# Head-wise expert routing on one Trainium2 core: three of eight blocks as a block diagonal, and transpositions dealt out between the expert blocks

## The chip, the cores and the metric

The kernel runs on one core of one Trainium2 chip. The metric is the device time of one execution in microseconds; lower is better. All data are fp32.

## What is computed

`x` has 64 x 1024 rows of 1024 numbers, seen as 16 heads of 64. Each row is routed to one head by the largest of 16 logits, and only that head is transformed and kept; all others are zero in the output.

```python
route_logits = x @ route_w                 # [B, S, 16]
best_head = np.argmax(route_logits, axis=-1)
x_heads = x.reshape(B, S, H, Dh)           # H = 16, Dh = 64
for h in range(H):
    mask = (best_head == h)
    out[:, :, h, :] = np.matmul(x_heads[:, :, h, :], experts[h]) * mask[:, :, None]
```

The kernel computes every head's product densely and multiplies by the mask.

## The kernel before

The 65536 rows are cut into 512 tiles of 128 rows (128 x 1024 fp32, 512 KB). SyncE's queue loads each tile into `xin` (20 buffers, line 87) and stores each output tile from `ot` (10 buffers, line 145). A tile's 1024 columns are eight blocks of 128, and each block holds two heads.

`transpose_tile` turns the eight blocks with TensorE (line 96), four into each of two PSUM buffers `ps_t`, and ScalarE copies each four to `xt` in SBUF (line 97). The transposed block is the stationary operand of the next step.

`expert_tile` takes each block `p` as four matmuls in 64x64 sub-arrays of TensorE (line 112): the upper and the lower 64 channels (two heads, `half`) times the first and the last 64 rows (`th`). The moving operand `mv` is 64 x 80: the head's 64x64 expert beside the 16 columns of `route_w` for those channels. Even blocks hold the expert first and then the routing columns, odd ones the other way round, so that the routing columns of a pair fall on the same 16 PSUM columns and add up there. Upper heads go to `ps_a` (two buffers, two banks each), lower heads to `ps_b` (one buffer, two banks). So 32 matmuls per tile.

Then VectorE adds up the partial logits (two reductions, line 120, and an addition, line 127), finds the maximum and its index (129, 131), makes the mask (133), and multiplies the upper heads from PSUM into `ot` (143). ScalarE copies the lower heads to `raw` (124), and GpSimd multiplies those into `ot` (144).

The order on TensorE follows the program: all eight transpositions of tile j, then all matmuls of tile j-1, and so on. The framework puts in the waits between engines from the buffers' use. Each fp32 expert matmul is recorded as two matmul records with a weight load each, a transposition as one.

Of the kernel before, what the change touches and what calls it, by code (L numbers as in the profile page):

```python
# [1 line left out]

# [5 lines left out]

FP32 = mybir.dt.float32
I32 = mybir.dt.int32  # L10
U32 = mybir.dt.uint32
ALU = mybir.AluOpType
AX = mybir.AxisListType

P = 128
XIN_BUFS = 20
OUT_BUFS = 10
XT_BUFS = 3


@with_exitstack
def kernel(
    ctx: ExitStack,
    tc: tile.TileContext,
    x: bass.AP,
    route_w: bass.AP,
    experts: bass.AP,
    out: bass.AP,
):

    nc = tc.nc
    B, S, D = x.shape  # L40
    H = experts.shape[0]
    Dh = D // H
    N = B * S
    NB = D // P
    NT = N // P
    HB = 512
    W = Dh + H
    assert D % P == 0 and N % P == 0 and Dh * H == D and 2 * Dh == P and NB == 8

    xg = x.rearrange("b s d -> (b s) d").rearrange("(g p) d -> g p d", p=P)  # L50
    og = out.rearrange("b s d -> (b s) d").rearrange("(g p) d -> g p d", p=P)

    consts = ctx.enter_context(tc.tile_pool(name="consts", bufs=1))
    small = ctx.enter_context(tc.tile_pool(name="small", bufs=3))
    xin_pool = ctx.enter_context(tc.tile_pool(name="xin", bufs=XIN_BUFS))
    xt_pool = ctx.enter_context(tc.tile_pool(name="xt", bufs=XT_BUFS))
    raw_pool = ctx.enter_context(tc.tile_pool(name="raw", bufs=3))
    out_pool = ctx.enter_context(tc.tile_pool(name="outp", bufs=OUT_BUFS))
    ps_t_pool = ctx.enter_context(tc.tile_pool(name="ps_t", bufs=2, space=bass.MemoryType.PSUM))
    ps_a_pool = ctx.enter_context(tc.tile_pool(name="ps_a", bufs=2, space=bass.MemoryType.PSUM))  # L60
    ps_b_pool = ctx.enter_context(tc.tile_pool(name="ps_b", bufs=1, space=bass.MemoryType.PSUM))

    ident = consts.tile([P, P], FP32, name="ident")
    make_identity(nc, ident)


    mv = consts.tile([P, NB, W], FP32, name="mv")
    ev = experts.rearrange("(q ab two) d e -> two ab d q e", two=2, ab=2)
    rv = route_w.rearrange("(q ab k) h -> ab k q h", k=P, ab=2)
    mvv = mv.rearrange("k (q ab) w -> k ab q w", ab=2)  # L70
    with nc.allow_non_contiguous_dma(reason="constants, once"):
        for ab in range(2):
            e0, r0 = (0, Dh) if ab == 0 else (H, 0)
            for half in range(2):
                nc.scalar.dma_start(
                    out=mvv[half * Dh:(half + 1) * Dh, ab, :, e0:e0 + Dh], in_=ev[half, ab])
            nc.scalar.dma_start(out=mvv[:, ab, :, r0:r0 + H], in_=rv[ab])  # L77


    hid_i = consts.tile([P, H], I32, name="hid_i")  # L80
    nc.gpsimd.iota(hid_i, pattern=[[1, H]], base=0, channel_multiplier=0)  # L81
    hid = consts.tile([P, H], FP32, name="hid")
    nc.vector.tensor_copy(out=hid, in_=hid_i)  # L83

    def load(j):
        xin = xin_pool.tile([P, D], FP32, name="xin", tag="xin")
        nc.sync.dma_start(out=xin, in_=xg[j])
        return xin

    def transpose_tile(xin):  # L90
        xt = xt_pool.tile([P, NB, P], FP32, name="xt", tag="xt")
        for half in range(2):
            ps_t = ps_t_pool.tile([P, NB // 2, P], FP32, name="ps_t", tag="ps_t")
            for q in range(NB // 2):
                p = half * (NB // 2) + q
                nc.tensor.transpose(ps_t[:, q, :], xin[:, p * P:(p + 1) * P], ident)  # L96
            nc.scalar.copy(out=xt[:, half * (NB // 2):(half + 1) * (NB // 2), :], in_=ps_t)  # L97
        return xt

    def windows(ps):  # L100

        return ps[:, :, 0:2 * W].rearrange("k q (ab w) -> k q ab w", ab=2)[:, :, :, 0:Dh]

    def expert_tile(j, xt):
        ps_a = ps_a_pool.tile([P, NB // 2, HB // 2], FP32, name="ps_a", tag="ps_a")
        ps_b = ps_b_pool.tile([P, NB // 2, HB // 2], FP32, name="ps_b", tag="ps_b")
        for p in range(NB):
            q, ab = divmod(p, 2)
            o0 = ab * Dh
            for half, ps in ((0, ps_a), (1, ps_b)):  # L110
                for th in range(2):
                    nc.tensor.matmul(  # L112
                        ps[th * 64:(th + 1) * 64, q, o0:o0 + W],
                        lhsT=xt[half * 64:(half + 1) * 64, p, th * 64:(th + 1) * 64],
                        rhs=mv[half * 64:(half + 1) * 64, p, :],
                        start=(p % 4 == 0), stop=(p % 4 == 3), skip_group_check=True)

        lg2 = small.tile([P, 2, H], FP32, name="lg2", tag="lg2")
        for half, ps in ((0, ps_a), (1, ps_b)):
            nc.vector.tensor_reduce(  # L120
                out=lg2[:, half, :], in_=ps[:, :, Dh:W].rearrange("k q h -> k h q"),
                op=ALU.add, axis=AX.X)
        raw = raw_pool.tile([P, NB // 2, 2, Dh], FP32, name="raw", tag="raw")
        nc.scalar.copy(out=raw, in_=windows(ps_b))  # L124

        lg = small.tile([P, H], FP32, name="lg", tag="lg")
        nc.vector.tensor_add(out=lg, in0=lg2[:, 0, :], in1=lg2[:, 1, :])  # L127
        mx = small.tile([P, 8], FP32, name="mx", tag="mx")
        nc.vector.max(out=mx, in_=lg)  # L129
        ix = small.tile([P, 8], U32, name="ix", tag="ix")  # L130
        nc.vector.max_index(out=ix, in_max=mx, in_values=lg)  # L131
        mask = small.tile([P, H], FP32, name="mask", tag="mask")
        nc.vector.tensor_scalar(  # L133
            out=mask, in0=hid, scalar1=ix[:, 0:1], scalar2=None, op0=ALU.is_equal)

        ot = out_pool.tile([P, D], FP32, name="ot", tag="ot")
        ov = ot.rearrange("k (q ab two e) -> k two q ab e", two=2, ab=2, e=Dh)
        mk = mask.rearrange("k (q ab two) -> k two q ab", two=2, ab=2)

        def bc(half):  # L140
            return mk[:, half].unsqueeze(3).to_broadcast([P, NB // 2, 2, Dh])

        nc.vector.tensor_tensor(out=ov[:, 0], in0=windows(ps_a), in1=bc(0), op=ALU.mult)  # L143
        nc.gpsimd.tensor_tensor(out=ov[:, 1], in0=raw, in1=bc(1), op=ALU.mult)  # L144
        nc.sync.dma_start(out=og[j], in_=ot)

    prev = None
    for j in range(NT + 1):
        xt = transpose_tile(load(j)) if j < NT else None
        if prev is not None:  # L150
            expert_tile(j - 1, prev)
        prev = xt


# [1 line left out]
_INS = ['x', 'route_w', 'experts']  # L156
_OUTS = [((64, 1024, 1024), 'float32')]


# [23 lines left out]
```

## Time and profile before

| what | value |
|---|---|
| median of 14 runs | 1646.59 us (1636.57 to 1663.43) |
| the profiled execution | 1641.88 us, its span 1640.1 us |
| TensorE, VectorE, ScalarE, GpSimd busy | 82%, 59%, 50%, 33% of the span |
| mean granted TensorE clock | 0.949 |
| data DMA (queue 1) | 536.94 MB, 90.8% of 16 engines' span |
| HBM traffic | 268.76 MB read, 268.44 MB written, 328 GB/s |

In the profile's rows PE is a matmul on TensorE and PEld a weight load, which can run beside it. DVE is VectorE, ACT ScalarE, POOL GpSimd, SP SyncE. L96 is line 96 of the kernel. "issue" is time in which an engine waited for nothing that the profile shows. The clock is the share of full TensorE clock that was granted.

### The profile page before, as it was taken

The numbers are of one execution on the slowest core, as the hardware profiler recorded it, in microseconds if no ns is written. First come the engines' busy times: TensorE is split into PE (matmuls) and PEld (weight loads), VectorE is DVE, ScalarE is ACT, GpSimd is POOL, SyncE is SP. The second block draws the span as 40 slices with busy tenths as digits, with TensorE's granted clock in tenths as the row PEclk, the third lists the DMA queues.
The fourth block names the chain that finished last, engine by engine and source line by source line (L and its number), as shares of the span: only waits on it lengthen the run. The fifth ranks groups of instructions, "written<-read, shape, count | busy, mean of one in ns | idle before, by whom it ended". The sixth has DMA issues, their size and how long they took to land.

```text
span 1640.1 us, 85016 instructions
## 1 busy us (share of the span) xinstructions
PE 1341.9 (82%) x36864; PEld 1168.6 (71%) x36864; DVE 965.2 (59%) x4097; ACT 812.5 (50%) x1537; POOL 537.6 (33%) x519
## 2 busy tenths in 40 slices
PE   7778888888888788788888888878878887888888
PEld 6667776767777677677777777767767776777777
DVE  4555555556556566565566565556555655656566
ACT  4444545445445555454455454545444544545555
POOL 2233333333333333333333333323333333333333
PEclk9899999999999999999999999999999999999999
DMA  9999999999999899999999999989999899999975
GB/s 348 352 359 362 328 344 328 320 340 337 317 332 356 314 347 355 335 334 334 338 339 344 337 337 334 337 310 330 324 332 343 322 310 345 356 313 338 340 257 208
DMA packets 149974, 542.70 MB, mean 331 GB/s; under 512 B 18528, under 2 KB 18528, under 8 KB 149600
## 3 DMA queue, kind: packets, MB, share of 16 engines
q1 hardware_dynamic: 147456, 536.94, 90.8%
q8 instruction: 290, 4.75, 1.2%
q14 instruction: 84, 0.69, 0.1%
q10 hardware_dynamic: 2144, 0.33, 0.1%
HBM read 268.76 MB, written 268.44 MB: 328 GB/s over the span
## 4 chain that ended last, share of the span: by engine, by line
PE 81%; issue 17%; ACT 1%; DVE 1%; DMA 0%; POOLq 0%; ACTq 0%; DVEq 0%
PE ps_t L96 34%; PE ps_a L112 27%; PE ps_b L112 20%; DVE lg L120 0%; ACT xt L97 0%; ACT raw L124 0%; DMA mv<-in_experts_dram 0%; ACT L97 0%; POOLq L178 0%; DVE lg L127 0%; DVE ix L131 0%; DVE mask L133 0%; DVE ot L143 0%; DVE mx L129 0%; ACTq L77 0%
## 5 line engine op out<-in xcount | busy, mean ns | idle before, releaser
L144 POOL TENSOR_TENSOR ot<-raw,mask 128x512 f32<-128x512 f32 x512 | 536.8, 1049 | 1098.3 <-ACT xt L97 857.4
L112 PE MATMUL ps_a<-mv,xt 64*64 64x80 f32 x16384 | 762.4, 241 | 119.4 <-issue 115.6
L112 PE MATMUL ps_b<-mv,xt 64*64 64x80 f32 x16384 | 756.8, 241 | 113.9 <-issue 109.4
L112 PEld LDWEIGHTS ps_a<-mv,xt 64*64 64x64 f32 x16384 | 651.1, 139 | 222.6 <-issue 145.9
L112 PEld LDWEIGHTS ps_b<-mv,xt 64*64 64x64 f32 x16384 | 646.3, 139 | 127.8 <-issue 122.9
L124 ACT COPY raw<-ps_b 128x512 f32<-128x512 f32 x512 | 300.2, 586 | 755.1 <-DVE lg L120 749.5
L96 PE MATMUL ps_t<-ident,xin 128*128 128x128 f32 x4096 | 600.0, 292 | 58.7 <-issue 52.3
L97 ACT COPY xt<-ps_t 128x512 f32<-128x512 f32 x1024 | 558.0, 596 | 61.4 <-PE ps_t L96 59.0
L96 PEld LDWEIGHTS ps_t<-ident,xin 128*128 128x128 f32 x4096 | 469.3, 148 | 114.8 <-issue 67.2
L120 DVE TENSOR_REDUCE lg<-ps_a 128x16 f32<-128x64 f32 x512 | 115.0, 225 | 508.9 <-PE ps_b L112 289.0
L143 DVE TENSOR_TENSOR ot<-ps_a,mask 128x512 f32<-128x512 f32 x512 | 354.0, 691 | 19.3 <-DVE mask L133 1.4
L133 DVE TENSOR_SCALAR mask<-hid,ix 128x16 f32<-128x16 f32 x512 | 119.9, 234 | 57.4 <-DVE ix L131 3.7
L120 DVE TENSOR_REDUCE lg<-ps_b 128x16 f32<-128x64 f32 x512 | 110.2, 215 | 31.3 <-PE ps_b L112 31.2
L129 DVE MAX8 mx<-lg 128x8 f32<-128x16 f32 x512 | 91.1, 178 | 17.6
L127 DVE TENSOR_TENSOR lg<-lg 128x16 f32<-128x16 f32 x512 | 89.8, 175 | 17.4
L131 DVE FIND_INDEX8 ix<-mx,lg 128x8 uint32<-128x16 f32 x512 | 86.3, 168 | 0.0
L131 DVE MATCH_VALUE_LOAD ix<-mx,lg 128x8 f32 x512 | 47.2, 92 | 17.7
L97 ACT ACT_TABLE_LOAD x1 | 1.3, 1283 | 5.9 <-DMA mv<-in_experts_dram 5.9
L83 DVE CAST hid<-hid_i 128x16 f32<-128x16 int32 x1 | 0.2, 239 | 1.1 <-POOL hid_i L81 1.1
masks.py:197 POOL MEMSET ident<- 128x128 f32 x1 | 0.2, 205 | 0.3 <-POOLq L167 0.3
masks.py:199 POOL TENSOR_SCALAR_AFFINE_SELECT ident<-ident 128x128 f32<-128x128 f32 x1 | 0.3, 292 | 0.0
L167 POOL MEMSET const-float32-0.0<- 128x1 f32 x1 | 0.1, 99 | 0.2 <-issue 0.2
(4 smaller groups left out, 0.4 us busy)
## 6 DMA issues: line engine op xcount, KB each, us to landing
xin<-in_x_dram SPq DMA_DIRECT2D x512, 512.0 KB, 5.9
out_dram<-ot SPq DMA_DIRECT2D x512, 512.0 KB, 5.7
mv<-in_experts_dram ACTq DMA_DIRECT2D x4, 64.0 KB, 6.4
mv<-in_route_w_dram ACTq DMA_DIRECT2D x2, 32.0 KB, 5.8
```

The costliest lines, as they stand in the source:

```text
L83: nc.vector.tensor_copy(out=hid, in_=hid_i)
L96: nc.tensor.transpose(ps_t[:, q, :], xin[:, p * P:(p + 1) * P], ident)
L97: nc.scalar.copy(out=xt[:, half * (NB // 2):(half + 1) * (NB // 2), :], in_=ps_t)
L112: nc.tensor.matmul(ps[th * 64:(th + 1) * 64, q, o0:o0 + W], lhsT=xt[half * 64:(half + 1) * 64, p, th * 64:(th + 1) * 64], rhs=mv[half * 64 ...
L120: nc.vector.tensor_reduce(out=lg2[:, half, :], in_=ps[:, :, Dh:W].rearrange("k q h -> k h q"), op=ALU.add, axis=AX.X)
L124: nc.scalar.copy(out=raw, in_=windows(ps_b))
L127: nc.vector.tensor_add(out=lg, in0=lg2[:, 0, :], in1=lg2[:, 1, :])
L129: nc.vector.max(out=mx, in_=lg)
L131: nc.vector.max_index(out=ix, in_max=mx, in_values=lg)
L133: nc.vector.tensor_scalar(out=mask, in0=hid, scalar1=ix[:, 0:1], scalar2=None, op0=ALU.is_equal)
L143: nc.vector.tensor_tensor(out=ov[:, 0], in0=windows(ps_a), in1=bc(0), op=ALU.mult)
L144: nc.gpsimd.tensor_tensor(out=ov[:, 1], in0=raw, in1=bc(1), op=ALU.mult)
```

## The change

Blocks 0 to 4 (`NS = 5`) stay as four 64x64 matmuls each. Blocks 5 to 7 (`NF = 3`) become one whole-array matmul each: the stationary operand is the transposed block, 128 x 128, and the moving operand `mf` is 128 x 144, the 16 routing columns beside a block diagonal of the two heads' experts, with zeros elsewhere. A tile's results take three PSUM banks, `ps_e`: upper heads, lower heads, and the three whole blocks; there are two such buffers, and `ps_t` has two banks as before.

The logits are added up by one VectorE reduction over all three banks. ScalarE copies both heads of the five blocks (2 x 352 columns) to `raw`, GpSimd multiplies these by the mask in two operations, and VectorE multiplies the three whole blocks.

The expert matmuls now run two tiles behind the transpositions (`LAG = 2`, four `xt` buffers), and the two are dealt out alternately: one expert block of tile j-2, one transposition of tile j, eight times per step.

```diff
-XT_BUFS = 3
+XT_BUFS = 4
+LAG = 2
...
-    ps_a_pool = ctx.enter_context(tc.tile_pool(name="ps_a", bufs=2, space=bass.MemoryType.PSUM))
-    ps_b_pool = ctx.enter_context(tc.tile_pool(name="ps_b", bufs=1, space=bass.MemoryType.PSUM))
+    ps_e_pool = ctx.enter_context(tc.tile_pool(name="ps_e", bufs=2, space=bass.MemoryType.PSUM))
...
+    mv = consts.tile([P, NS, W], FP32, name="mv")
+    mf = consts.tile([P, NF, STEP], FP32, name="mf")
+    nc.vector.memset(mf, 0.0)
...
+    def transposes(xin, xt):
         for half in range(2):
             ps_t = ps_t_pool.tile([P, NB // 2, P], FP32, name="ps_t", tag="ps_t")
             for q in range(NB // 2):
                 p = half * (NB // 2) + q
                 nc.tensor.transpose(ps_t[:, q, :], xin[:, p * P:(p + 1) * P], ident)
+                if q == NB // 2 - 1:
+                    nc.scalar.copy(out=xt[:, half * (NB // 2):(half + 1) * (NB // 2), :], in_=ps_t)
+                yield
...
+    def experts_pass(ps, xt):
+        for p in range(NS):
+            s, ab = divmod(p, 2)
+            o0 = s * STEP + ab * Dh
+            for half in range(2):
                 for th in range(2):
                     nc.tensor.matmul(
+                        ps[th * 64:(th + 1) * 64, half, o0:o0 + W],
                         lhsT=xt[half * 64:(half + 1) * 64, p, th * 64:(th + 1) * 64],
                         rhs=mv[half * 64:(half + 1) * 64, p, :],
+                        start=(p == 0), stop=(p == NS - 1), skip_group_check=True)
+            yield
+        for f in range(NF):
+            o0 = f * STEP + Dh
+            nc.tensor.matmul(
+                ps[:, 2, o0:o0 + STEP], lhsT=xt[:, NS + f, :], rhs=mf[:, f, :],
+                start=(f == 0), stop=(f == NF - 1), skip_group_check=True)
+            yield
...
+    def finish(j, ps):
+        lg = small.tile([P, H], FP32, name="lg", tag="lg")
+        parts = ps[:, :, 0:SLOTS * STEP].rearrange("k b (s w) -> k b s w", w=STEP)
+        nc.vector.tensor_reduce(
+            out=lg, in_=parts[:, :, :, Dh:W].rearrange("k b s h -> k h b s"),
+            op=ALU.add, axis=AX.XY)
+        RW = (NS // 2) * STEP + Dh
+        raw = raw_pool.tile([P, 2, SLOTS * STEP], FP32, name="raw", tag="raw")
+        nc.scalar.copy(out=raw[:, :, 0:RW], in_=ps[:, 0:2, 0:RW])
...
+        nc.vector.tensor_tensor(
+            out=ov[:, NS:], in1=bc(mk[:, NS:]), op=ALU.mult,
+            in0=ps[:, 2, W:W + NF * STEP].rearrange("k (f w) -> k f w", w=STEP)[:, :, 0:2 * Dh]
+            .rearrange("k f (two e) -> k f two e", two=2))
+        rv4 = raw.rearrange("k two (s w) -> k s two w", w=STEP)
+        for ab in range(2):
+            n = (NS + 1 - ab) // 2
+            o0 = ab * W
+            nc.gpsimd.tensor_tensor(
+                out=ov[:, ab:NS:2], in0=rv4[:, 0:n, :, o0:o0 + Dh], in1=bc(mk[:, ab:NS:2]),
+                op=ALU.mult)
         nc.sync.dma_start(out=og[j], in_=ot)
...
+    for j in range(NT + LAG):
+        tr = mm = iter(())
+        if j < NT:
+            xin = load(j)
+            xts[j] = xt_pool.tile([P, NB, P], FP32, name="xt", tag="xt")
+            tr = transposes(xin, xts[j])
+        if j >= LAG:
+            ps = ps_e_pool.tile([P, SLOTS, HB], FP32, name="ps_e", tag="ps_e")
+            mm = experts_pass(ps, xts.pop(j - LAG))
+        for _ in range(NB):
+            next(mm, None)
+            next(tr, None)
+        if j >= LAG:
+            finish(j - LAG, ps)
```

`W` is 80, `STEP` is 144, `SLOTS` is 3, `HB` is 512 and `NB` is 8.

## The prediction

> **What bounds the kernel now.** I read the page first: engines, chain of waits, groups, queues.
>
> ```profile
> PE 1341.9 (82%) x36864; PEld 1168.6 (71%) x36864; DVE 965.2 (59%) x4097; ACT 812.5 (50%) x1537; POOL 537.6 (33%) x519
> ...
> q8 instruction: 290, 4.75, 1.2%
> ...
> PE 81%; issue 17%; ACT 1%; DVE 1%; DMA 0%; POOLq 0%; ACTq 0%; DVEq 0%
> ...
> L112 PE MATMUL ps_a<-mv,xt 64*64 64x80 f32 x16384 | 762.4, 241 | 119.4 <-issue 115.6
> ...
> L96 PE MATMUL ps_t<-ident,xin 128*128 128x128 f32 x4096 | 600.0, 292 | 58.7 <-issue 52.3
> ```
>
> The chain is TensorE and its own "issue" idle time; every other engine has slack. A transposition is one matmul record (4096 = 512 x 8), an expert matmul two (16384 = 512 x 16 x 2, and as many in ps_b). So a tile has 72 matmul records, and as many weight loads.
>
> Next the timeline, TensorE alone, where the two kinds of work meet. Columns: start, length, instruction, count.
>
> ```profile
> 803.96 0.23 PE L112 MATMUL ps_a<-mv,xt 64*64 64x80 f32 x1
> 803.97 0.24 PE L112 MATMUL ps_b<-mv,xt 64*64 64x80 f32 x2
> 804.14 1.09 PE L96 MATMUL ps_t<-ident,xin 128*128 128x128 f32 x8
> 805.16 0.29 PE L112 MATMUL ps_a<-mv,xt 64*64 64x80 f32 x2
> ```
>
> ```profile
> 808.36 0.29 PE L112 MATMUL ps_a<-mv,xt 64*64 64x80 f32 x2 [0.70 <-DVE mask L133]
> 808.37 0.29 PE L112 MATMUL ps_b<-mv,xt 64*64 64x80 f32 x2
> 808.42 0.29 PE L112 MATMUL ps_a<-mv,xt 64*64 64x80 f32 x2
> 808.49 0.23 PE L112 MATMUL ps_b<-mv,xt 64*64 64x80 f32 x1
> 808.49 0.23 PE L112 MATMUL ps_a<-mv,xt 64*64 64x80 f32 x1
> 808.50 0.23 PE L112 MATMUL ps_b<-mv,xt 64*64 64x80 f32 x1
> ```
>
> I took all start-to-start distances from the trace's records. Within a form at full clock, transpositions follow each other at 0.109 us, and four 64x80 matmuls, one per sub-array, take 0.069. Where the form changes it is slower, and equally so at nearly every change. From the last expert matmul's start to the first transposition is 0.160 (it would be 0.067 if the next could follow); from the last transposition to the first expert matmul is 0.202 (against 0.107). So about 0.095 is lost on leaving a form, in both directions. On entering one, the first weights are not there yet: the first transposition takes 0.166 instead of 0.109 (0.057 more), and the first eight expert matmuls of a phase start within 0.140 where nothing else is waited for (second fence; the median is 0.196, because ps_b then still waits for the copy of raw). A change of form costs some 0.15. Now there are two per tile.
>
> A tile without stalls is 1.022 (transpositions to first expert matmul) + 1.269 = 2.291 us; 512 of them are 1173. The matmuls span 1629 us. The other 456 are 348 us of gaps over 0.3 us, 84 lost in 168 us at half clock, and the wait on raw. The gaps come 127 matmuls, or a multiple, apart: 73,728 TensorE instructions over 290 packets of the instruction queue is 254 per packet, so these are waits for code. Successive gap ends one block apart lie 4.4 to 7.4 us from each other, median 5.9.
>
> Last, windows: busy per engine, clock, DMA share, GB/s.
>
> ```profile
> 668.21:671.62 3.41, 0.40 (x21) 0.24 (x11) 0.35 (x2) 0.01 (x1) 0.58 (x1) 1.00 0.96 370
> 671.62:675.03 3.41, 3.39 (x45) 2.92 (x49) 1.75 (x7) 1.76 (x3) 1.05 (x1) 0.50 0.21 68
> 1590.00:1600.00 10.00, 10.00 (x316) 8.81 (x311) 8.21 (x34) 6.50 (x14) 4.64 (x5) 1.00 0.60 233
> 800.00:1000.00 200.00, 165.51 (x4539) 144.50 (x4533) 118.97 (x505) 100.39 (x190) 66.84 (x64) 0.94 0.94 338
> ```
>
> A window with a code wait is followed by one at half clock. At the end, when the loads are over, 316 matmuls pass in 10 us: 2.28 us per tile, as computed.
>
> **The change, part by part.** Call T a transposition, E a block of four 64x64 matmuls (eight records), F one 128x144 matmul (two records). The new order is E0 T0 E1 T1 E2 T2 E3 T3 E4 T4 F0 T5 F1 T6 F2 T7, again and again. T and F use the whole array, so five E islands stand alone: ten changes of form per tile instead of two.
>
> - Each E island: 0.140 from first to last start + 0.160 out = 0.300; five are 1.500. In its phase now an E costs 0.138. The wait on raw is gone, as ps_e has two buffers: the low value.
> - T0 to T3 stand alone: 0.057 + 0.202 = 0.259 each; four are 1.036.
> - F has no row. The streams give 0.069/80 = 0.86 ns and 0.109/128 = 0.85 ns per column, so 144 columns take 0.123 per record, six records 0.738. Bounds: 0.109 (T, as if columns cost nothing) to 0.180 (its weight load exposed as at an entry); I take 0.123, because T's row, with weights of the same size, shows them hidden.
> - The stretch T4 to T7: 0.057 in, three T at 0.109, F 0.738, and T7 0.202: 1.324.
>
> Sum: 1.500 + 1.036 + 1.324 = 3.860 us per tile. Streaming alone is 8 x 0.109 + 5 x 0.138 + 0.738 = 2.30, so 1.56 is changes of form.
>
> A step between T and F, six per tile, I count at nothing: both are 128*128, and the rows change cost only where the form does; passing among the four sub-arrays costs none (0.069 for four). The other bound is 0.15 each, 0.90 per tile. The Trainium skill (TensorEngine Tiling (Array Packing), Key Properties) says that a change of tiling mode drains the TensorE, not a change of tile; by it T and F, in one mode, pass freely, which no row here can show, and the sum stays 3.860.
>
> Code waits: 54 records per tile are 108 instructions instead of 144, so one packet lasts 254/108 = 2.35 tiles, 9.1 us. The longest turn-around seen is 7.4 (and 4.2 us of work plus the longest gap, 3.95, is 8.1), at 331 GB/s; the new pace asks for 1.05 MB per 3.86 us, 272. I count no code wait.
>
> Clock: from the windows, half clock follows where matmuls streamed for up to 1.29 us of 3.41, transpositions included, and never where they streamed longer. The new order streams 2.30/3.86 of 3.41 = 2.03. So full clock. The Trainium skill (TensorE: Matmul & The Clock Gate, Part 4) says that transpositions don't count as busy for this clock; that speaks against thinning the other matmuls out (to 1.26 of 3.41). In this trace windows are told apart better with transpositions counted than without. At half clock the sum would be 3.86 + 2.30 = 6.16.
>
> Other engines per tile: ACT two copies of 0.596 and one of 704 elements (0.586 x 704/512 = 0.81): 2.0. DVE one reduction of 144 elements (0.225 to 0.5), four steps of 0.67 together, a product of 384 (0.52 to 0.69): at most 1.9. GpSimd 640 elements in two operations at 1049/512 ns each: 1.3 to 2.1. All under 3.86, and ps_e lets them lag a whole tile. xt has a tile more slack. On SyncE a load still waits for transpositions 20 tiles back, a store for both products, in the old order; nothing queues there at a slower pace. The extra constants' DMAs land beside the first two tiles' transpositions.
>
> Time: 510 x 3.860 = 1968.6; 7.9 to the first transposition (as now); two tiles transposed alone at half clock, 16 x 0.213 = 3.4; two tiles of E and F alone, 1.7 each; 2.8 after the last matmul (as now). Span 1986.1; the execution is 1.8 longer than the span now (1641.9 against 1640.1): 1988 us. The profiled run is 0.3% under the median of the runs shown; I leave that out, since the spread came from code waits.
>
> **Rivals.**
> 1. Faster: the changes of form are hidden, say because a lone T's drain overlaps the next E's load. It needs a price below (3.18 - 2.30)/10 = 0.088 each, where I read 0.15. At zero, code (5.9 us per 2.35 tiles: 2.5) or DMA bounds it: 1.05 MB at the 388 GB/s of 30 to 40 us is 2.7 us per tile, about 1400 us. Against: 0.160 and 0.202 hardly vary over 500 tiles. 0.05.
> 2. T and F drain each other too: +0.90 per tile, 2450. No row excludes it. 0.10.
> 3. Code waits stay: 348 us in 238 gaps, 1.46 each, per 2.35 tiles: +0.62, 2305. Against: the stretches with fewer loads. 0.08.
> 4. Half clock: 3165. 0.02.
>
> **How the numbers follow.** My forecast has 0.74, a result near the old time 0.01. Its own range: F at 0.109 takes 43 off; T's entries hidden would take 5 x 0.057 x 510 = 145 off, of which I allow a third; E islands at the median 0.196 add 143. So 1900 to 2130, which also holds the smaller sizes of rivals 2 and 3. About 0.5% is what can be told from no change: faster 0.05, same 0.01, slower 0.94.
>
> **What would show it.** Right: the "issue" share of the chain falls to a few per cent, the clock is near 1.0, a lone T is 0.26 from the next E, an E island 0.30 from the next T, F records 0.12 apart. Wrong: weight loads of the next form starting before the last matmul has drained (rival 1); 0.2 or more between T and F (2); gaps every 127 matmuls (3); clock 0.5 (4).

## The result, and the profile after

The changed kernel takes 1996.4 us in the median of ten runs (1994.7 to 1999.1); it is slower, at 1.217 times the kernel before, 95% interval 1.2137 to 1.2203. Its profiled execution took 1996.2 us, the span 1994.4.

From the page of the changed kernel: busy time, the code queue, the chain, and TensorE's three groups of matmuls.

```profile
PE 1979.9 (99%) x27648; PEld 1404.8 (70%) x27648; DVE 780.4 (39%) x3074; ACT 934.6 (47%) x1537; POOL 720.3 (36%) x1031
...
q8 instruction: 218, 3.57, 0.8%
...
PE 99%; DMA 0%; ACT 0%; ACTq 0%; DVE 0%; POOL 0%; issue 0%; POOLq 0%
...
L110 PE MATMUL ps_t<-ident,xin 128*128 128x128 f32 x4096 | 1258.7, 308 | 7.9 <-DMA xin<-in_x_dram 4.6
...
L121 PE MATMUL ps_e<-mv,xt 64*64 64x80 f32 x20480 | 944.6, 255 | 0.2 <-DVE ot L159 0.2
...
L129 PE MATMUL ps_e<-mf,xt 128*128 128x144 f32 x3072 | 576.3, 287 | 0.0
```

There are a quarter fewer matmul records (27648 against 36864) and a quarter less code (218 packets against 290). "issue" has gone from 17% of the chain to nothing, and TensorE is the chain from end to end. Yet it takes longer: the matmuls wait for next to nothing that the waits show (the weight loads of `ps_e` have 94.6 us of "issue", one short wait per tile), and still do not follow each other closely. Where the time is, the timeline of TensorE shows, one tile of it (start, length, instruction, count):

```profile
1000.15 0.33 PE L110 MATMUL ps_t<-ident,xin 128*128 128x128 f32 x1
1000.41 0.37 PE L121 MATMUL ps_e<-mv,xt 64*64 64x80 f32 x8
1000.71 0.33 PE L110 MATMUL ps_t<-ident,xin 128*128 128x128 f32 x1
...
1002.38 0.33 PE L110 MATMUL ps_t<-ident,xin 128*128 128x128 f32 x1
1002.55 0.41 PE L129 MATMUL ps_e<-mf,xt 128*128 128x144 f32 x2
1002.79 0.27 PE L110 MATMUL ps_t<-ident,xin 128*128 128x128 f32 x1
...
1003.51 0.27 PE L110 MATMUL ps_t<-ident,xin 128*128 128x128 f32 x1
1003.71 0.37 PE L121 MATMUL ps_e<-mv,xt 64*64 64x80 f32 x8
1004.01 0.33 PE L110 MATMUL ps_t<-ident,xin 128*128 128x128 f32 x1
```

From the start of a lone transposition to the next matmul's start is 0.26 us (1000.15 to 1000.41), and from an expert block in 64x64 tiles to the next transposition 0.30 (1000.41 to 1000.71). In a row they cost 0.109 and 0.138. The stretch from 1002.38 to 1003.71, with transpositions and whole blocks in turn, has such a loss only at its two ends. A tile takes 3.860 us from 1000.15 to 1004.01; the 1st and the 99th percentile of all tiles are both 3.86.

The windows view over 200 us, in the same columns as before, has the granted clock at 1.00 and the data at 273 GB/s:

```profile
800.00:1000.00 200.00, 200.00 (x2803) 141.99 (x2799) 78.64 (x309) 94.07 (x156) 73.07 (x104) 1.00 0.76 273
```

A "busy" share of 100% here is no sign of a good use of TensorE: the row of a lone transposition (0.33) reaches past the start of the next matmul (0.26 later), so the time lost between the two counts as busy.

### The profile page after: what moved, and what is told of

Its sections match the earlier page's. It is cut to its first block, busy times and chain, and to the rows that moved or that the text cites. A ratio compares the mean times of both kernels' runs of the same rounds, so it can differ in the third digit from the quotient of the medians.

```text
span 1994.4 us, 65582 instructions
## 1 busy us (share of the span) xinstructions
PE 1979.9 (99%) x27648; PEld 1404.8 (70%) x27648; DVE 780.4 (39%) x3074; ACT 934.6 (47%) x1537; POOL 720.3 (36%) x1031
## 4 chain that ended last, share of the span: by engine, by line
PE 99%; DMA 0%; ACT 0%; ACTq 0%; DVE 0%; POOL 0%; issue 0%; POOLq 0%
PE ps_t L110 42%; PE ps_e L121 38%; PE ps_e L129 19%; DMA mv<-in_experts_dram 0%; ACT raw L142 0%; ACT L112 0%; POOL ot L167 0%; ACTq L84 0%; DVE lg L137 0%; ACTq L88 0%; ACTq L91 0%; ACT xt L112 0%; POOLq L212 0%; DVE ot L159 0%; DVE mx L145 0%
## 5 line engine op out<-in xcount | busy, mean ns | idle before, releaser
L110 PE MATMUL ps_t<-ident,xin 128*128 128x128 f32 x4096 | 1258.7, 308 | 7.9 <-DMA xin<-in_x_dram 4.6
L167 POOL TENSOR_TENSOR ot<-raw,mask 128x384 f32<-128x384 f32 (+1 forms) x1024 | 719.5, 723 | 1270.0 <-ACT raw L142 1141.2
L121 PE MATMUL ps_e<-mv,xt 64*64 64x80 f32 x20480 | 944.6, 255 | 0.2 <-DVE ot L159 0.2
L121 PEld LDWEIGHTS ps_e<-mv,xt 64*64 64x64 f32 x20480 | 532.4, 131 | 340.9 <-issue 94.6
L110 PEld LDWEIGHTS ps_t<-ident,xin 128*128 128x128 f32 x4096 | 571.4, 140 | 242.0 <-issue 5.9
L129 PE MATMUL ps_e<-mf,xt 128*128 128x144 f32 x3072 | 576.3, 287 | 0.0
L137 DVE TENSOR_REDUCE lg<-ps_e 128x16 f32<-128x144 f32 x512 | 157.5, 308 | 997.3 <-PE ps_e L129 997.3
L129 PEld LDWEIGHTS ps_e<-mf,xt 128*128 128x128 f32 x3072 | 492.4, 200 | 0.2
L142 ACT COPY raw<-ps_e 128x704 f32<-128x704 f32 x512 | 384.4, 751 | 2.4 <-DVE lg L137 2.3
L159 DVE TENSOR_TENSOR ot<-ps_e,mask 128x384 f32<-128x384 f32 x512 | 285.5, 558 | 121.3 <-ACT raw L142 121.1
```

The costliest lines, as they stand in the source:

```text
L121: nc.tensor.matmul(ps[th * 64:(th + 1) * 64, half, o0:o0 + W], lhsT=xt[half * 64:(half + 1) * 64, p, th * 64:(th + 1) * 64], rhs=mv[half * ...
L129: nc.tensor.matmul(ps[:, 2, o0:o0 + STEP], lhsT=xt[:, NS + f, :], rhs=mf[:, f, :], start=(f == 0), stop=(f == NF - 1), skip_group_check=True)
L137: nc.vector.tensor_reduce(out=lg, in_=parts[:, :, :, Dh:W].rearrange("k b s h -> k h b s"), op=ALU.add, axis=AX.XY)
L142: nc.scalar.copy(out=raw[:, :, 0:RW], in_=ps[:, 0:2, 0:RW])
L159: nc.vector.tensor_tensor(out=ov[:, NS:], in1=bc(mk[:, NS:]), op=ALU.mult, in0=ps[:, 2, W:W + NF * STEP].rearrange("k (f w) -> k f w", w=S ...
L167: nc.gpsimd.tensor_tensor(out=ov[:, ab:NS:2], in0=rv4[:, 0:n, :, o0:o0 + Dh], in1=bc(mk[:, ab:NS:2]), op=ALU.mult)
```

## The experiments

The theory is that each change between the 64x64 form and the whole-array form costs some 0.15 us, wherever it stands. The rivals are that the whole-array blocks, the banks or the lag are slow; that alternating is dear in itself; and that only what stands alone is dear. In what follows T is a transposition, E a block of four 64x64 matmuls and F a whole-array block, as in the prediction. The orders e1, e2, e7 and e8 keep the changed kernel's matmuls (27648 records each) and only move them.

**Two changes of form per tile: all E, all F, all T (e1).**

```diff
         for _ in range(NB):
             next(mm, None)
+        for _ in range(NB):
             next(tr, None)
```

> The changed kernel with its alternation undone: per step all five E blocks, then F0 to F2, then T0 to T7; blocks, banks and lag as in the changed kernel. Two changes of form per tile instead of ten. If a change of form costs 0.15 us: E stretch 0.140 + 4 x 0.138 / 2 x 2 streams = 0.692 to its last start, 0.160 out; F and T together 0.057 + 6 x 0.124 + 7 x 0.109 + 0.202; 2.62 us per tile on TensorE, 1360 us if nothing else binds. Then two other bounds are near: data at 388 GB/s 2.70 us per tile (1400 us), and code waits come back, since a code packet lasts only 2.35 x 2.6 = 6.1 us against turn-arounds of 4.4 to 7.4. I expect 1380 to 1560 us, with issue gaps 127 matmuls apart. Rival: the whole-array blocks, the three banks or the lag are what is slow; then it stays above 1800 us.

1386.3 us, 0.839 times the kernel before (interval 0.833 to 0.845). So what is slow is neither the blocks, nor the banks, nor the lag: with the alternation taken away, the rest of the change is a gain of 16%, and this version beats both kernels. From its page (busy, the data queue, HBM, the chain):

```profile
PE 1367.2 (99%) x27648; PEld 1232.4 (89%) x27648; DVE 781.0 (56%) x3074; ACT 884.0 (64%) x1537; POOL 721.5 (52%) x1031
...
q1 hardware_dynamic: 147456, 536.94, 99.0%
...
HBM read 268.76 MB, written 268.44 MB: 388 GB/s over the span
...
PE 98%; DMA 1%; issue 0%; DVE 0%; ACTq 0%; POOL 0%; ACT 0%; POOLq 0%; DVEq 0%
```

The count of matmuls is the changed kernel's, the busy time 613 us less. From the 1st to the 90th percentile a tile takes 2.658 us; I had 2.62. The 0.04 more is the entry into the whole-array form through an F: its second record comes 0.226 after its first, 0.103 more than in a row, where a transposition has 0.057. The code waits that I expected did not come: ten gaps over 0.3 us, none 127 matmuls after another. The data queue is at 99%, so the data may be next in line; no run here tests that for e1.

**Six changes (e2) and four (e7).**

```diff
-        for _ in range(NB):
-            next(mm, None)
-            next(tr, None)
+        for run in (2, 2, 1, 1, 1, 1):              # e2
+            for _ in range(run):
+                next(mm, None)
+            for _ in range(run):
+                next(tr, None)
```

In e7 the runs are (3, 4), (2, 1), (1, 1), (1, 1), (1, 1) of blocks and transpositions.

> The changed kernel with the order E0 E1 T0 T1, E2 E3 T2 T3, E4 T4 F0 T5 F1 T6 F2 T7: six changes of form per tile, all else as it is. If each change costs its 0.15 us whatever stands between: 2 x 0.438 + 0.300 + 2 x 0.368 + 1.324 = 3.24 us per tile, 510 x 3.24 + 26 = 1676 us, and next to no code wait (a packet lasts 7.6 us): 1665 to 1720 us. Rival: what costs is that transpositions and expert blocks alternate at all (the T and F stretch is unchanged here), or a drain whose size depends on what stands alone: no such drop in proportion, above 1800 us.

> The changed kernel with four changes of form per tile: E0 E1 E2, T0 to T3, E3 E4, T4 F0 T5 F1 T6 F2 T7. If the price per change is constant, the time lies on the line through ten, six and two changes: 0.140 + 2 x 0.138 + 0.160 = 0.576, 0.057 + 3 x 0.109 + 0.202 = 0.586, 0.438, 1.324 give 2.92 us per tile, 510 x 2.92 + 26 = 1517 us (1505 to 1540). Rival: the price depends on how much stands alone (a lone transposition is dear, four in a row are free): then it is nearer to the 1386 us of two changes, under 1450.

e2 took 1680.6 us (1.0175 times the kernel before, 1.010 to 1.025), e7 1522.2 (0.928, 0.920 to 0.935), both inside what I expected and outside what the rivals asked for (above 1800, under 1450). Their tiles take 3.240 and 2.930 us in the median.

**Two changes, transpositions and F in turn (e8).**

```diff
-        for _ in range(NB):
-            next(mm, None)
-            next(tr, None)
+        for e, t in ((NS, 1), (1, 1), (1, 1), (1, NB)):
+            for _ in range(e):
+                next(mm, None)
+            for _ in range(t):
+                next(tr, None)
```

> The changed kernel with E0 to E4 in a row and then T0 F0 T1 F1 T2 F2 T3 to T7: transpositions and whole-array blocks still alternate, but only within their form; two changes of form per tile. If a change between T and F is free: E 0.852, then 0.057 + 3 x 0.246 + 7 x 0.109 + 0.202 = 1.760, 2.61 us per tile on TensorE, 1360 us; data may hold it at 2.65 us or so: 1355 to 1395 us. Rival: alternating in itself costs 0.15 at each of six steps more: 3.5 us per tile, 1810 us.

1429.6 us (0.870, 0.862 to 0.877): outside what I expected, though far from the rival's 1810. The undisturbed tiles, nearly a quarter of all, take 2.617 us, as computed, so T and F do alternate for nothing; in the timeline a T after the first takes 0.11 us before an F, and an F (two records) 0.25 before a T, as in a row:

```profile
801.82 0.33 PE L110 MATMUL ps_t<-ident,xin 128*128 128x128 f32 x1
801.99 0.41 PE L129 MATMUL ps_e<-mf,xt 128*128 128x144 f32 x2
802.24 0.27 PE L110 MATMUL ps_t<-ident,xin 128*128 128x128 f32 x1
802.35 0.41 PE L129 MATMUL ps_e<-mf,xt 128*128 128x144 f32 x2
```

But the median tile takes 2.747. The waits say on what:

```profile
DVE ot L159 <- DMA out_dram<-ot: 464.0, 403, 2.2
...
PEld ps_e L121 <- DVE ot L159: 128.3, 395, 1.4
```

VectorE waits 403 times for an output buffer, that is for a store to land, and TensorE then waits 395 times for `ps_e`. The stores bind here. Why the data moved at some 380 GB/s in this kernel and at some 395 in e1 stays open.

Four orders, with a tile's time undisturbed: two changes 2.617 (e8), four 2.930 (e7), six 3.240 (e2), ten 3.860 (the changed kernel). The steps are 0.313, 0.310 and 0.620, that is 0.156, 0.155 and 0.155 per change: a straight line, which meets zero changes at 2.306. The streams alone were worked out as 2.30. The price does not depend on how much stands between. It does depend on what comes first after the change: the line holds for orders that enter the whole-array form through a T, and e1, which enters through an F, lies 0.04 above it.

**No change of form at all: eight whole blocks (e3, e5).** In e3, `NS = 0`, with all blocks through `mf`:

```diff
-    NS = 5
+    NS = 0
...
+            b, s = divmod(f, SLOTS)
+            o0 = s * STEP + Dh
             nc.tensor.matmul(
-                ps[:, 2, o0:o0 + STEP], lhsT=xt[:, NS + f, :], rhs=mf[:, f, :],
+                ps[:, b, o0:o0 + STEP], lhsT=xt[:, f, :], rhs=mf[:, f, :],
```

> All eight blocks go through the whole array as block diagonals (NS = 0), alternated one by one with the transpositions as in the changed kernel: no change of form at all, sixteen F records per tile. Two VectorE reductions and an addition instead of one reduction; ScalarE copies six blocks for GpSimd, VectorE multiplies two. If only changes of form cost: 8 x 0.109 + 16 x 0.124 = 2.86 us per tile on TensorE, 1480 us, unless data at 388 GB/s (2.70 us) or other engines (ScalarE 2.2, VectorE 1.6, GpSimd 1.6 us) bind; 48 instructions per tile, so no code waits: 1470 to 1540 us. Rival: alternating costs by itself: 0.15 on each of sixteen steps, 5.2 us per tile, 2680 us; or half that, 2070 us.

1792 us (1.084, 1.070 to 1.097): a miss, and not by the theory's cause. The trace has another order than the program, made by the framework when it orders each engine's instructions: on SyncE's queue mostly 2 to 6 loads were issued ahead of the stores, where the changed kernel has 15 to 23, and on TensorE the alternation holds only in places (there a T follows an F record after 0.122 and an F a T after 0.109, as in a row). TensorE waited 166 us for `xin`. So the time of e3 decides nothing. e5 issues the loads twelve tiles ahead in the program:

```diff
-            xin = load(j)
+        for i in range(0 if j == 0 else j + AHEAD, min(j + AHEAD + 1, NT)):   # AHEAD = 12
+            xins[i] = load(i)
```

> The kernel with all eight blocks through the whole array, but with every load issued twelve tiles ahead in the program, so that twelve loads or more stand ahead of the stores on SyncE's queue (there were 2 to 6). If loads held up behind stores were what made it slow: 2.86 us per tile on TensorE, 1470 to 1540 us, and hardly any wait on xin. Rival: whole-array records cost more than 0.123 us, or another engine binds: it stays near 1790 us.

1650.5 us (1.007, 1.004 to 1.011), above the 1470 to 1540 that I expected: the loads were a part, and something else binds. The waits say where:

```profile
PEld ps_t L103 <- ACT xt L105: 175.6, 370, 0.5
PE ps_t L103 <- ACT xt L105: 87.9, 369, 0.2
```

In 370 of 512 tiles the transpositions wait some 0.5 us for ScalarE to empty `ps_t`. ScalarE is not short of time: it is busy for 59% of the span, and before the copy that they wait for it had itself been idle, waiting for TensorE:

```profile
801.93 0.71 PE L103 MATMUL ps_t<-ident,xin 128*128 128x128 f32 x5
802.24 1.08 ACT L105 COPY xt<-ps_t 128x512 f32<-128x512 f32 x2 [1.44 <-PE ps_t L103]
802.88 0.33 PE L103 MATMUL ps_t<-ident,xin 128*128 128x128 f32 x1 [0.24 <-ACT xt L105]
803.04 1.64 PE L112 MATMUL ps_e<-mf,xt 128*128 128x144 f32 x12
```

The order is at fault here too. For some 113 tiles near the start the trace keeps the program's order, T and F in strict turn, and a tile takes 2.853 us, against 2.86 worked out. After that the order is mostly another: twelve F records in a row, and six transpositions in a row, of which the last begins the next tile. Four transpositions fill one buffer of `ps_t` in 0.44 us, the copy of the other takes 0.59, and a tile takes 3.300. So F's price holds, and the tiles in strict turn show once more that changing between T and F costs nothing.

**How fast the data can move (e4, e6).** All matrix work is left out: each tile is loaded, copied by VectorE and stored; in e6 the loads are twelve tiles ahead, by the same edit as in e5.

```diff
+    for j in range(NT):
+        xin = load(j)
+        ot = out_pool.tile([P, D], FP32, name="ot", tag="ot")
+        nc.vector.tensor_copy(out=ot, in_=xin)
+        nc.sync.dma_start(out=og[j], in_=ot)
```

> Leaves out all matrix work: each tile is loaded, copied by VectorE and stored, with the same queues and buffers. It gives the floor that the data movement sets. At 388 GB/s (the rate before between 30 and 40 us) 1.05 MB per tile is 2.70 us, 1384 us and some 10 at the ends; at the 417 GB/s of the loads alone 1290 us. I expect 1290 to 1450 us. If it is above 1600 us, data movement and not TensorE held the kernel before, and undoing the changes of form brings little.

> Leaves out all matrix work, as the copy before did, but with the loads twelve tiles ahead of the stores on SyncE's queue. If the copy at 1588 us was held by loads queued behind stores, this runs at 395 GB/s or more, the rate that the grouped order reached: 1300 to 1375 us. Rival: a pure copy can't go faster, because loads and stores disturb each other: near 1590 us.

e4 took 1588 us, above the 1450 that I expected at most, and e6 1294, in one run each. In e4 three loads, three stores and again three loads were issued in turn, and the queue's own waits show the loads behind stores that wait for the copy:

```profile
SPq L176 <- DVE ot L175: 1006.9, 510, 5.4
```

With the loads ahead, the HBM line of e6's page stands at 416 GB/s over the span. So these 537 MB can move in 1294 us, and the rate of the data did not hold the kernel before (TensorE waited for `xin` once there, 4.3 us at the start); e1 is 7% above 1294.

**What the code waits hang on (e9, e10).** e9 is e1 with six blocks in 64x64 tiles and two whole; e10 is the kernel before with half its loads.

```diff
-    NS = 5
+    NS = 6                                          # e9
...
-        xt = transpose_tile(load(j)) if j < NT else None
+        if j < NT and j % 2 == 0:                   # e10
+            xin = load(j)
+        xt = transpose_tile(xin) if j < NT else None
```

> The grouped order (two changes of form per tile) with six blocks in 64x64 tiles and two through the whole array; the logits are reduced in two steps and added. TensorE alone: 0.830 + 0.160, then 0.103 + 4 x 0.1225 + 7 x 0.109 + 0.202 = 2.55 us per tile, 0.11 less than with five. A tile has 120 TensorE instructions instead of 108, so a code packet lasts 254/120 x 2.55 = 5.4 us, against 6.25 with five and turn-arounds of 4.4 to 7.4, median 5.9, in the kernel before. If the code waits come from that race, gaps 127 matmuls apart return, some 0.5 us or more per packet: 1385 to 1470 us, no gain over five. Rival: the gaps have another cause that the new blocks removed; then no gaps, and data or TensorE sets 1330 to 1370 us.

> The kernel before, with only every second tile loaded; the odd tile takes the same input again (half of the input traffic is left out). All TensorE work, instructions and stores are as before. If the waits for code come from data traffic on the same DMA engines, most of the 348 us of gaps go, and the half clock with them: 1190 to 1300 us (2.29 to 2.5 us per tile). Rival: a code packet takes its time whatever the data do: gaps stay at 1.2 us per 1.76 tiles, and the time within 5% of 1640 us.

e9 took 1401.5 us (0.847, 0.840 to 0.853). Its undisturbed tile is 2.551 us, 0.107 less than e1's, but it is no faster: 89 gaps over 0.3 us are back, 71 us in all, and 93% of the distances between them are 127 matmuls or a multiple, give or take one. The longest of the waits of TensorE:

```profile
PE ps_e L121 <- issue: 39.3, 62, 1.6
```

e10 took 1412.6 us (0.853, 0.844 to 0.861), between the two theories: the gaps fell from 348 us in 238 to 148 us in 149, and the time at half clock from 168 to 40 us, with the data at 292 GB/s on average. So half of the loads account for a good half of these waits; with all the stores and the other loads left, more of them stay than I had expected, and what the rest hangs on stays open.

## Why the prediction was right

- **The order on TensorE and the count of changes.** Ten per tile, and they set the time. Undoing them (e1) gives 610 us back.
- **Price of a change.** 0.095 out and some 0.055 in were read from the two changes per tile of the kernel before. The changed kernel has the same distances, 0.258 for a lone T (0.259 worked out) and 0.300 for an E island, and the line through four orders gives 0.155.
- **T and F at nothing.** Right: in the changed kernel a transposition follows an F record after 0.122, and an F a transposition after 0.109. The Trainium skill (TensorEngine Tiling (Array Packing), Key Properties) says that changing the tiling mode, and not just the tile, drains TensorE; these distances agree with it. Rival 2 is out.
- **F's record.** 0.123 worked out, 0.122 and 0.125 measured. Its entry, 0.103 where it comes first, was not in the sum, as a T comes first there.
- **Code waits at nothing.** Right: ten gaps over 0.3 us, 7.4 us in all, against 348 before. e9 shows how near they were in e1: at 5.4 us per code packet the gaps return, at 6.25 (e1) there were none; the changed kernel has 9.1. Rival 3 is out.
- **Full clock.** 1.00. Matmuls streamed for 2.03 of 3.41 us with transpositions and 1.26 without, by the prediction's figures; in the kernel before, half clock followed up to 1.3 with them and 1.1 without. The Trainium skill (TensorE: Matmul & The Clock Gate, Part 4) says that transpositions don't count as busy for this clock; the new streams are above both marks, so this run does not test that.
- **Other engines.** The reduction took 0.308, the product of 384 0.558, the copy to `raw` 0.751, GpSimd's two operations 1.45 per tile: all inside their bounds or under them, and hidden.
- **Rival 1** held that the changes could be hidden, at a price below 0.088; the price is 0.155. The first weight load of the next form starts 0.157 us after the last expert matmul's start, and 0.200 after the last transposition's (0.256 after a lone one), in the kernel before and after, and the same in e2 and e7: none starts earlier. The sign as I put it, a load before the last matmul has drained, can't be read from the rows: their ends are modelled, and every such load starts 0.07 before the modelled end, in the kernel before too.

The sum was 1986 for the span, and the span is 1994. The tile was right to the nanosecond (3.860), in part by luck, as terms that were off by 1 to 4 ns cancel; so the 8 us are the ends. I mis-sized three terms there. The first loop step began at 12.87 us, not 11.3, since ScalarE waited 7.9 us for its constants (5.9 before) before it could copy `xt`; I had put these at nothing. Nor is 7.9 the time of the first transposition in the kernel before: that starts at 4.31, and the second tile's at 7.87, now at 9.85. Two loop steps then ran wholly or partly at half clock, at 6.48 and 4.22 us: 3.0 more. And after the last matmul starts there are 6.6 us to the end of the span, not 2.8; before there were 6.4, and I had misread the end of the trace.

## What to carry to other kernels

Count the changes between sub-array tiles and the whole array on TensorE, and lay the work out so that each form runs in one stretch: here each change cost 0.155 us, more than a 128x128 transposition (0.109), and 1.24 us of 3.86 per tile came from eight avoidable ones. Read the price from the few changes that the kernel already makes, as start-to-start distances, before dealing two kinds of work out alternately; the waits and idle times showed hardly any of it afterwards, since the rows of two matmuls overlap across the loss. And if a change has two parts, try them apart: the whole-array blocks with their banks and lag were worth 16% here, and the alternation took more than all of it away.

## What was not expected of the hardware

Loads and stores together can move at 416 GB/s over a whole span (e6), where the kernel before showed 331 and I took 388 as the limit. The order on one DMA queue moved a plain copy from 1294 to 1588 us. And 0.11 us per tile of faster compute (e9 against e1) was paid back in full in code waits, which came when TensorE used a packet up in 5.4 us and not when it took 6.25. That this is a race between a packet's arrival and TensorE's pace is argued, not shown: the gap ends one block apart in e9 lie 5.7 to 7.4 us from each other, and why e1 then has none stays open.
